# Four plain chunks, an early norm and tables in pieces: a change at the start of a two-layer decoder trunk

## The chip, the cores and the metric

The kernel runs on one core of a Trainium2 chip. The metric is device time in microseconds (us) of one execution of the whole program; the median over several runs counts. The engines are TensorE (PE, with its weight loads PEld), VectorE (DVE), ScalarE (ACT), GpSimd (POOL) and SyncE (SP). SP, ACT and POOL also issue transfers (DMA). Every engine works through its own queue in order.

## The reference

The reference is a decoder trunk of two layers (D = 1024, sequence 512, float32). Cut to what matters here, a layer is:

```python
h = h + 0.5 * swiglu(rmsnorm(h, ffn1_norm[l]), w_gate, w_up, w_down)   # D_FF = 2816
z = rmsnorm(h, mix_norm[l]) @ w_in[l]                                  # four mixers on slices of z:
h = h + concat[MLA(z), SpatialGate(z), HGRN2(z), Retention(z)] @ w_out[l]
h = h + 0.5 * swiglu(rmsnorm(h, ffn2_norm[l]), w_gate, w_up, w_down)
h = h + (p[l] @ w_proj) * sigmoid(rmsnorm(h, ple_norm[l]) @ w_gate)
```

with `swiglu(x) = (silu(x @ w_gate) * (x @ w_up)) @ w_down`, and a final rmsnorm. MLA and Retention turn their queries and keys by sines and cosines of the positions; these are the tables of this study.

## The kernel before

**Layout and number format.** The residual stream lies transposed, as eight tiles `h[k]` of 128 x 512. Each float32 operand is split into a high part (a cast on ACT, L138 or L219) and a low part (a subtraction on DVE, L139 or L220); a product is three matmuls, high-high, high-low and low-high (L190 to L192, function `mm3`). So each weight block costs a load, a cast and a subtraction ahead of its matmuls.

**Feed-forward stage** (`ffn`, L360). Four such stages, two in each layer. D_FF is worked off in 22 chunks of 128 columns, in groups of 4, 4, 4, 4 and 6. A chunk computes gate and up, then silu(gate) times up times the norm's factor, and splits that into `hid`. Most chunks (class `Chunk`, L372) compute gate and up together by a scheme of seven half-width products (named 1 to 7, method `go`) in place of eight, on weight sums made by `seven` (L160) and on the right factors, sums and differences of halves of the normed input that `Right.add` (L275) makes through `Norm.add7` (L323). Product 1 uses only the plain input. The seven weight blocks of a chunk come from four loads: `s1` and `s3` (256 KB each, and POOL adds a second block to each while loading, L174 and L175), `raw` (512 KB, tile `wr`) and `a22` (256 KB). A chunk of seven products is 84 matmuls of 256 columns. The first two chunks of the program are plain: 48 matmuls of 512 columns each, gate into one bank of PSUM and up into another (L428 to L440). Their epilogue starts at L435, where DVE multiplies the bank by the norm's factor `r` into a tile `g` and so frees the bank; Silu (L436) and three DVE steps follow. There are four banks for these products (tag `d`): chunks 0 and 1 hold all four.

**Down products** (`downs`, L413). From the second group on, the products with w_down of the group before (12 matmuls of 512 columns for each of eight `m`) are put between the products of the chunks (`step`), one or two or three to a chunk.

**The start** (L1136 to L1175). `h[k]` and the weights of chunk 0 are loaded in turns on SP, in an order written out by a chain (`inturn`), then the weights of chunk 1, then the constants `cs`. The loads of the seven-product chunks of the first stage wait for `cs` (`start[1]`). The sum of squares for the norm grows on the way (L336 to L343); its last step is at 20.19 us. After that the program has the eight `add7` calls for the right factors and then `ffn`, whose first line is the norm: `norm.scale()` casts the sum (L243), subtracts (L244), adds over the partitions with two matmuls (L247), and takes the inverse root by Ln, Exp (L258, L259) and one Newton step on DVE (L236 to L238).

**Tables** (`tables`, L484). Called once, in the first stage, after chunk 9 (L462). It loads the positions (`pin`), casts them to a side tile `posf`, makes three sines (`sine`, L490: nine steps on DVE and one Sin on ACT each, L493 to L501), loads two decay tables (`dec`, L513), makes four products (L516), and some masks.

**What sets the order.** The program is written as one long text; a planner at build time gives each engine its queue. An instruction's rank is its place in the text, and what stands under `urgent()` ranks 6000 places earlier (weights, their splits, the norm, the chunk's copies out of PSUM). Of the instructions whose inputs and tiles are there, the first in rank goes first. Tiles come from rings with a fixed number of places, named by a tag; the tiles of one tag are handed out in the order of the text, each as soon as a place is free. Rings that matter here: `t` (six places of 128 x 512: `xg` of the right factors, `g` and `u` of the chunks, `a22`, the norm's `ac`, `rv` and `rt`, all temporary tiles of the tables), `side` (four places: `s1`, `s3`, `posf`), `w` (six split weight tiles), `st` (four, also split weights) and `raw` (three). `after` and `inturn` add an order between two instructions without a wait for data.

## Time and profile before

| | us |
|---|---|
| median of 3 runs | 2148.11 (2147.02 to 2150.12) |
| profiled execution | 2146.84 |
| its span in the profile | 2145.1 |
| PE busy | 2078.9 |
| DVE busy | 1599.0 |
| ACT busy | 1061.8 |
| POOL busy | 171.1 |

The profile is one execution. The difference between the span and the execution's own time, 1.7 us, lies outside the recorded instructions. A row of the timeline gives start, duration, engine, line of the kernel, operation, the tile written and the tiles read, the shapes and a count; in brackets stands how long the engine was idle before and what released it. A row of a stretch gives busy time and count for each engine, then the granted clock of PE (1.00 is full), the busy share of the DMA engines and their GB/s. Matmuls overlap, so the distance of their starts tells more than their durations. The same holds, less strongly, for DVE and ACT.

### The profile page before, as it was taken

What the parts mean: (1) busy time and instruction counts of PE and PEld (TensorE: products, weight loads), DVE (VectorE), ACT (ScalarE), POOL (GpSimd) and SP (SyncE); (2) the same over time, 40 slices, a digit from 0 to 9 for tenths busy, and PEclk for the clock granted to TensorE, in tenths of its full rate; (3) what the DMA queues carried; (4) which work ended last, traced back from release to release, by engine and by line L of the source; (5) the groups of instructions that cost most, each with busy time, mean ns of one, the idle gap of its engine ahead of it and who ended that gap; (6) DMA issues with size and microseconds to landing.
All of it is one profiled execution on the core that took longest, in us unless ns stands there. A gap on an engine that the chain in (4) does not pass through costs nothing.

```text
span 2145.1 us, 36254 instructions
## 1 busy us (share of the span) xinstructions
PE 2078.9 (97%) x14336; PEld 1821.7 (85%) x14336; DVE 1599.0 (75%) x2720; ACT 1061.8 (50%) x1897; POOL 171.1 (8%) x217
## 2 busy tenths in 40 slices
PE   6997999999999999999989999999999999999997
PEld 5996999877678999998889999988776889998987
DVE  7778776776678877777897776777765887777676
ACT  7443444643566544444664444455445664444452
POOL 1101110001000111110010111000010010011000
PEclk8998999999999999999999999999999999999999
DMA  6635563323234655564355566432222465565341
GB/s 190 154 122 146 138 156 85 113 82 95 64 89 118 163 152 153 147 153 111 116 143 152 145 157 153 121 101 95 66 89 69 114 153 152 143 154 151 98 132 52
DMA packets 119561, 267.47 MB, mean 125 GB/s; under 512 B 13024, under 2 KB 17632, under 8 KB 119392
## 3 DMA queue, kind: packets, MB, share of 16 engines
q1 hardware_dynamic: 90928, 215.15, 31.7%
q0 software_dynamic: 25792, 47.20, 13.7%
q10 hardware_dynamic: 2672, 2.82, 0.4%
q8 instruction: 112, 1.84, 0.4%
q14 instruction: 57, 0.47, 0.1%
HBM read 260.92 MB, written 2.10 MB: 123 GB/s over the span
## 4 chain that ended last, share of the span: by engine, by line
PE 87%; DVE 6%; DMA 3%; ACT 3%; issue 1%; SPq 0%; ACTq 0%; DVEq 0%
PE dn L190 8%; PE dn L192 7%; PE gx L190 7%; PE gx L192 7%; PE gx L191 7%; PE dn L191 7%; PE gy L190 5%; PE gy L191 5%; PE gy L192 5%; PE z L190 3%; PE z L191 3%; PE z L192 3%; DMA wr<-in_wgu 1%; PE y L190 1%; PE y L192 1%; PE y L191 1%
## 5 line engine op out<-in xcount | busy, mean ns | idle before, releaser
L138 ACT CAST ws<-wr 128x512 fp32r<-128x512 f32 x344 | 210.6, 621 | 386.4 <-DMA wr<-in_wgu 191.3
L190 PE MATMUL gx<-b,ws 128*128 128x256 f32 x1296 | 368.7, 285 | 19.2 <-ACT g L389 9.1
L191 PE MATMUL gx<-b,ws 128*128 128x256 f32 x1296 | 367.3, 283 | 0.0
L192 PE MATMUL gx<-b,ws 128*128 128x256 f32 x1296 | 367.1, 283 | 0.0
L139 DVE TENSOR_TENSOR ws<-wr,ws 128x512 fp32r<-128x512 f32 x344 | 233.9, 688 | 134.3 <-ACT ws L138 133.7
L139 DVE TENSOR_TENSOR wl<-wr,wh 128x1024 fp32r<-128x1024 f32 (+3 forms) x197 | 222.4, 1131 | 149.0 <-PE gy L192 78.9
L138 ACT CAST wh<-wr 128x1024 fp32r<-128x1024 f32 (+3 forms) x197 | 191.9, 975 | 198.6 <-PE z L191 63.2
L190 PE MATMUL dn<-hid,wh 128*128 128x512 f32 x704 | 281.0, 399 | 0.9 <-ACT wh L138 0.5
L192 PE MATMUL dn<-hid,wl 128*128 128x512 f32 x704 | 279.3, 398 | 0.0
L191 PE MATMUL dn<-hid,wh 128*128 128x512 f32 x704 | 275.0, 392 | 0.0
L190 PEld LDWEIGHTS gx<-b,ws 128*128 128x128 f32 x1296 | 248.8, 192 | 27.0 <-ACT u L393 10.0
L190 PE MATMUL gy<-b,ws 128*128 128x256 f32 x872 | 249.3, 286 | 5.4 <-DVE g L398 4.1
L191 PEld LDWEIGHTS gx<-b,ws 128*128 128x128 f32 x1296 | 248.8, 192 | 3.5
L191 PE MATMUL gy<-b,ws 128*128 128x256 f32 x872 | 248.0, 284 | 1.7 <-DVE b L139 1.7
L192 PEld LDWEIGHTS gx<-b,ws 128*128 128x128 f32 x1296 | 248.8, 192 | 0.1
L192 PE MATMUL gy<-b,ws 128*128 128x256 f32 x872 | 247.1, 284 | 1.3 <-DVE ws L139 1.3
L190 PEld LDWEIGHTS gy<-b,ws 128*128 128x128 f32 x872 | 168.4, 193 | 8.0 <-DVE g L398 4.7
L191 PEld LDWEIGHTS gy<-b,ws 128*128 128x128 f32 x872 | 168.5, 193 | 3.3 <-DVE b L139 1.9
L192 PEld LDWEIGHTS gy<-b,ws 128*128 128x128 f32 x872 | 168.1, 193 | 2.9 <-DVE ws L139 1.5
L192 PEld LDWEIGHTS dn<-hid,wl 128*128 128x128 f32 x704 | 132.3, 188 | 34.4 <-DVE wl L139 3.3
L190 PEld LDWEIGHTS dn<-hid,wh 128*128 128x128 f32 x704 | 132.8, 189 | 33.1 <-ACT wh L138 8.1
L191 PEld LDWEIGHTS dn<-hid,wh 128*128 128x128 f32 x704 | 132.9, 189 | 24.9
(379 smaller groups left out, 4260.3 us busy)
## 6 DMA issues: line engine op xcount, KB each, us to landing
s<-in_wgu SPq DMA_DIRECT2D x172, 256.0 KB, 2.8
wr<-in_wgu SPq DMA_DIRECT2D x86, 512.0 KB, 4.4
s<-in_wgu POOLq DMA_DIRECT2D x172, 256.0 KB, 4.9
wr<-in_wdn SPq DMA_DIRECT2D x64, 512.0 KB, 4.8
a<-in_wgu SPq DMA_DIRECT2D x86, 256.0 KB, 4.3
wr<-in_winT SPq DMA_DIRECT2D x40, 512.0 KB, 3.5
wr<-in_wdn SPq DMA_DIRECT2D x32, 384.0 KB, 3.2
wr<-in_winN SPq DMA_DIRECT2D x16, 512.0 KB, 3.5
```

Of the source, the lines that this page charges most:

```text
L138: i = act.copy(hi, src)
L139: dve.tensor_tensor(lo, src, hi.bitcast(F32), op=ALU.subtract)
L190: i = pe.matmul(o, lhsT=a[0], rhs=b[0], start=start, stop=False, skip_group_check=go_on)
L191: pe.matmul(o, lhsT=a[0], rhs=b[1], start=False, stop=False, skip_group_check=go_on)
L192: pe.matmul(o, lhsT=a[1], rhs=b[0], start=False, stop=stop, skip_group_check=go_on)
```

## The change

1. **Four plain chunks.** In the first stage of the program chunks 0 to 3 are plain, not only 0 and 1. Chunks 2 and 3 load and split their gate and up blocks by `weights` (512 KB each, two blocks a chunk); the cast of chunk 2's second block is put behind the norm's Exp on ACT (`late`). The loads have no wait of their own. In `seven` the argument `late` goes away.
2. **The norm ahead of the right factors.** `norm.scale()` is called before the `add7` calls; in them, for this first norm alone, the scaled copy `xg` is put behind the norm's Exp on ACT. `ffn` takes the result from `norm.r`.
3. **Tables in pieces.** `tables` becomes a generator, of which the stage takes a piece after each odd chunk from 5 on: the sine for MLA, the cosine, its two products with the decay, the sine, its two products, the masks. A sine has its own load and cast of the positions; `posf` goes away, and the decay tables are loaded twice. The memset of the upper half of `tabM` moves to the start.
4. **a22 in the ring of the sums.** `a22` is taken from `side`, which gets five places; `t` gets five.

```diff
     def t2(shape=(P, T), dt=F32, name="t"):
-        return tp.tile(list(shape), dt, tag="t", bufs=6, name=nm(name))
+        return tp.tile(list(shape), dt, tag="t", bufs=5, name=nm(name))
...
+    tabs = {"m": cp.tile([P, T], F32, name="tabM")}
+    pool.memset(tabs["m"][0:64], 1.0)
...
     def side(shape=(P, T), name="sd"):
-        return tp.tile(list(shape), F32, tag="side", bufs=4, name=nm(name))
+        return tp.tile(list(shape), F32, tag="side", bufs=5, name=nm(name))
...
-    def weights(src, cols=WB, keep=False, two=False, one=False):
+    def weights(src, cols=WB, keep=False, two=False, one=False, late=None):
...
-            parts(hi[:, :cols], lo[:, :cols], raw[:, :cols])
+            inturn(parts(hi[:, :cols], lo[:, :cols], raw[:, :cols]), late)
             return hi, lo
 
-    def seven(a1, a2, wait=None, late=None):
+    def seven(a1, a2, wait=None):
...
-            s1, s3, raw, a22 = side(name="s1"), side(name="s3"), rtile(), t2(name="a22")
+            s1, s3, raw, a22 = side(name="s1"), side(name="s3"), rtile(), side(name="a22")
...
-            for p, src in ((7, s3), (4, a22)):
-                inturn(keep(p, src), late)
+            keep(7, s3)
+            keep(4, a22)
             dve.tensor_tensor(r2, r2, r1, op=ALU.add)
-            inturn(keep(3, r2), late)
+            keep(3, r2)
...
             g = t2(name="xg")
-            act.activation(g, h[k], AF.Copy, scale=gain(self.gi, k))
-            if plain is None:
+            i = act.activation(g, h[k], AF.Copy, scale=gain(self.gi, k))
+            if plain is not None:
+                after(i, self.exp)
+            else:
                 self.square(k)
...
-        r = norm.scale()
+        r = norm.r or norm.scale()
...
-                if start and f < 2:
+                if start and f < 4:
                     o = []
                     for m in range(2):
                         o.append(start[0].pop(0) if f == 0 else dense("gu"))
-                        for k in range(KD if f else 0):
-                            mm3(o[m], wpart(start[2][m], k * P), xpart(norm.x[k]), k == 0, k == KD - 1)
+                        if f > 0:
+                            w = start[2][m] if f == 1 else weights(wgu[idx, f, m], late=norm.exp if f == 2 and m else None)
+                            for k in range(KD):
+                                mm3(o[m], wpart(w, k * P), xpart(norm.x[k]), k == 0, k == KD - 1)
...
-                if f == 9 and hook is not None:
-                    hook()
+                if hook is not None and f % 2:
+                    next(hook, None)
...
+    def sine(dst, p0, inv, phase, turn):
+        q = slice(p0, P)
+        pin, a, n = t2((P, T), I32, name="pin"), t2(name="ang"), t2(name="turn")
+        nc.scalar.dma_start(out=pin, in_=pos)
+        pick = lambda c: cs[q, c:c + 1] if isinstance(c, int) else c
+        a, n, dst = a[q], n[q], dst[q]
+        dve.tensor_copy(n, pin[q])
+        dve.tensor_scalar(a, n, pick(inv), None, op0=ALU.mult)
...
+        act.activation(dst, a, AF.Sin)
 
     def tables():
...
+        sine(tabs["m"], 64, 0, 1, 2)
+        dve.tensor_scalar(tabs["m"][64:P], tabs["m"][64:P], cs[64:P, 3:4], None, op0=ALU.mult)
+        yield
+        for nme, phase, turn in (("c", 5, 6), ("s", 0.0, 0.0)):
+            for s in "qk":
+                tabs[nme + s] = cp.tile([P, T], F32, name=f"tab{nme}{s}")
+            tq = tabs[nme + "q"]
+            sine(tq, 0, 4, phase, turn)
+            yield
+            for j, s in ((1, "k"), (0, "q")):
+                dt_ = t2(name="dec")
+                nc.scalar.dma_start(out=dt_, in_=dec[j])
+                dve.tensor_tensor(tabs[nme + s], tq, dt_, op=ALU.mult)
+            yield
...
     start[1] = inturn(nc.sync.dma_start(out=cs, in_=cst[:, 0:K_TOP]), prev)
+    norm.scale()
     for k in PAIRED:
         norm.add7(k, norm.x)
     for l in range(L):
         nxt = Norm(4 * l + V_MIX)
-        ffn(2 * l, norm, nxt.add, *((start, tables) if l == 0 else ()))
+        ffn(2 * l, norm, nxt.add, *((start, tables()) if l == 0 else ()))
```

More of the change, by code (lines that the diff above doesn't have):

```diff
@@ L165, in keep @@
             w[p] = (wtile("ws") if n else spare("ws"))[:, 0:WB].rearrange("p (e c) -> p e c", e=2)
-            return parts(w[p][:, 0], w[p][:, 1], src)
+            parts(w[p][:, 0], w[p][:, 1], src)
         with urgent():
-            s1, s3, raw, a22 = side(name="s1"), side(name="s3"), rtile(), t2(name="a22")
+            s1, s3, raw, a22 = side(name="s1"), side(name="s3"), rtile(), side(name="a22")
             r1, r2 = raw[:, 0:T], raw[:, T:WB]
@@ L316, in __init__ @@
             self.x = [None] * KD
-            self.acc = None
+            self.acc = self.r = None
         def add(self, k):
@@ L375, in __init__ @@
             def __init__(self, f):
-                late = norm.exp if start and f == 2 else None
-                self.w = seven(wgu[idx, f, 0], wgu[idx, f, 1], start and start[1], late)
+                self.w = seven(wgu[idx, f, 0], wgu[idx, f, 1], start and start[1])
                 X, yz = dense("gx"), dense("gy")
@@ L479, in ffn @@
             done(m)
-    tabs = {}
-    def tables():
-        pin = t2((P, T), I32, name="pin")
-        posf = side(name="posf")
-        nc.scalar.dma_start(out=pin, in_=pos)
-        dve.tensor_copy(posf, pin)
-        def sine(dst, inv, phase, turn):
-            a, n = t2(name="ang"), t2(name="turn")
-            dve.tensor_scalar(a, posf, inv, None, op0=ALU.mult)
-            dve.tensor_scalar(n, a, 1.0 / TWO_PI, turn, op0=ALU.mult, op1=ALU.add)
-            dve.tensor_scalar(n, n, MAGIC, None, op0=ALU.add)
-            dve.tensor_scalar(n, n, MAGIC, None, op0=ALU.subtract)
-            for c in (C1, C2, C3):
-                dve.scalar_tensor_tensor(a, n, -c, a, op0=ALU.mult, op1=ALU.add)
-            dve.tensor_scalar(a, a, phase, PI_LO, op0=ALU.add, op1=ALU.min)
-            dve.tensor_scalar(a, a, -PI_LO, None, op0=ALU.max)
-            act.activation(dst, a, AF.Sin)
-        tm = cp.tile([P, T], F32, name="tabM")
-        sine(tm, cs[:, 0:1], cs[:, 1:2], cs[:, 2:3])
-        dve.tensor_scalar(tm, tm, cs[:, 3:4], None, op0=ALU.mult)
-        pool.memset(tm[0:64], 1.0)
-        tabs["m"] = tm
-        co, si = t2(name="co"), t2(name="si")
-        sine(co, cs[:, 4:5], cs[:, 5:6], cs[:, 6:7])
-        sine(si, cs[:, 4:5], 0.0, 0.0)
-        for j, s in enumerate("qk"):
-            dt_ = t2(name="dec")
-            nc.scalar.dma_start(out=dt_, in_=dec[j])
-            for nme, src in (("c", co), ("s", si)):
-                tb = cp.tile([P, T], F32, name=f"tab{nme}{s}")
-                dve.tensor_tensor(tb, src, dt_, op=ALU.mult)
-                tabs[nme + s] = tb
@@ new lines, in sine @@
+    def sine(dst, p0, inv, phase, turn):
[6 more added lines that the diff above has]
+        dve.tensor_scalar(a, n, pick(inv), None, op0=ALU.mult)
+        dve.tensor_scalar(n, a, 1.0 / TWO_PI, pick(turn), op0=ALU.mult, op1=ALU.add)
+        dve.tensor_scalar(n, n, MAGIC, None, op0=ALU.add)
+        dve.tensor_scalar(n, n, MAGIC, None, op0=ALU.subtract)
+        for c in (C1, C2, C3):
+            dve.scalar_tensor_tensor(a, n, -c, a, op0=ALU.mult, op1=ALU.add)
+        dve.tensor_scalar(a, a, pick(phase), PI_LO, op0=ALU.add, op1=ALU.min)
+        dve.tensor_scalar(a, a, -PI_LO, None, op0=ALU.max)
+        act.activation(dst, a, AF.Sin)
```

## The prediction

> **What bounds the kernel now.** I read the page first (engines, chain), then the list of PE's waits, then busy time by stretches, then the start and the stage of the tables in order of time.
>
> ```profile
> PE 2078.9 (97%) x14336; PEld 1821.7 (85%) x14336; DVE 1599.0 (75%) x2720; ACT 1061.8 (50%) x1897; POOL 171.1 (8%) x217
> PE 87%; DVE 6%; DMA 3%; ACT 3%; issue 1%; SPq 0%; ACTq 0%; DVEq 0%
> ```
>
> PE is 97% busy and sets the end; it is idle for 66 of 2145.1 us. The longest waits of PE:
>
> ```profile
> PE ms L247 <- ACT ac L243: 9.2, 1, 9.2
> PE gx L190 <- ACT g L389: 9.1, 2, 8.2
> PE gx L190 <- DVE g L435: 6.6, 1, 6.6
> ```
>
> The first and the third make one pause at the start; the second lies in the stage of the tables. Stretches of the start (busy time of PE, PEld, DVE, ACT, POOL, granted clock, DMA share, GB/s), and a full stretch to compare:
>
> ```profile
> 0.00:25.00 25.00, 23.17 (x100) 17.26 (x101) 16.74 (x30) 18.85 (x34) 4.51 (x12) 1.00 0.92 295
> 28.90:46.47 17.57, 1.58 (x2) 0.57 (x2) 17.21 (x39) 12.46 (x26) 1.75 (x3) 0.57 0.38 87
> 46.47:52.02 5.55, 5.55 (x26) 5.55 (x27) 4.67 (x9) 4.71 (x9) 0.85 (x1) 0.52 0.39 61
> 100.00:125.00 25.00, 25.00 (x172) 23.08 (x171) 16.98 (x27) 11.41 (x21) 2.60 (x3) 1.00 0.52 144
> ```
>
> From 28.90 to 46.47 PE does two small matmuls while DVE is busy for 17.21 of 17.57 us: **the pause at the start is DVE's work**, not a transfer. Behind it the clock is at half: 26 matmuls take 5.55 us.
>
> **The start, part by part.** PE's end of chunk 1 and start of chunk 2, then five matmuls around a gap in the stage of the tables, which show the distance of their starts:
>
> ```profile
> 28.28 0.39 PE L191 MATMUL gu<-x,wh 128*128 128x512 f32 x1
> 28.51 0.39 PE L192 MATMUL gu<-x,wl 128*128 128x512 f32 x1
> 46.47 0.58 PE L190 MATMUL gx<-x,ws 128*128 128x256 f32 x1 [6.58 <-DVE g L435]
> ...
> 166.09 0.28 PE L191 MATMUL gy<-x,ws 128*128 128x256 f32 x1
> 166.21 0.28 PE L192 MATMUL gy<-x,ws 128*128 128x256 f32 x1
> 167.74 0.51 PE L192 MATMUL gy<-b,ws 128*128 128x256 f32 x1 [1.25 <-DVE ws L139]
> 168.25 0.41 PE L191 MATMUL gy<-b,ws 128*128 128x256 f32 x1
> 168.47 0.41 PE L192 MATMUL gy<-b,ws 128*128 128x256 f32 x1
> ```
>
> 512 columns take 0.23, 256 columns 0.12, and 0.21 at half clock. The 26 behind the pause lose 5.55 - 26 x 0.12 = 2.4. What releases chunk 2 is L435, the first step of chunk 0's epilogue, which frees a bank of sums:
>
> ```profile
> 20.19 0.69 DVE L343 TENSOR_TENSOR acc<-acc,sq 128x512 f32<-128x512 f32 x1
> 33.13 0.68 DVE L139 TENSOR_TENSOR b<-xg,b 128x512 fp32r<-128x512 f32 x1
> 33.74 0.41 DVE L294 SCALAR_TENSOR_TENSOR xg<-xg,xg 128x256 f32<-128x256 f32 x1
> 34.07 0.42 DVE L139 TENSOR_TENSOR b<-xg,b 128x256 fp32r<-128x256 f32 x1
> 34.50 1.42 ACT L326 ACTIVATE xg<-h,vec 128x512 f32<-128x512 f32 x2
> 37.47 0.62 ACT L243 CAST ac<-acc 128x512 fp32r<-128x512 f32 x1
> 41.38 0.63 ACT L259 ACTIVATE r<-rt 128x512 f32<-128x512 f32 x1
> 44.19 0.69 DVE L238 SCALAR_TENSOR_TENSOR r<-rt,r 128x512 f32<-128x512 f32 x1
> 45.73 0.69 DVE L435 TENSOR_TENSOR g<-gu,r 128x512 f32<-128x512 f32 x1
> L139 DVE TENSOR_TENSOR wl<-wr,wh 128x1024 fp32r<-128x1024 f32 (+3 forms) x197 | 222.4, 1131 | 149.0 <-PE gy L192 78.9 <-ACT wh L138 36.1 <-ACT g L391 29.8
> ```
>
> The sum of squares is ready at 20.88, but the norm begins at 37.47, behind the last two xg at 34.50: ring t is handed out in program order, and the right factors stand first. The change turns this round, so r comes early. But chunk 0's g is a tile of the same ring that comes after all eight xg, and on DVE its step stands behind theirs. So I count what DVE does before L435, at the distance of starts seen in these rows: 0.60 for 512 columns, 0.33 for 256, 1.13 for 1024.
>
> - The norm takes 4.5 us from 37.47 to the end of Exp at 42.01. It starts at 20.9 plus a shift. Chunk 2's first block (512 KB) has no wait on its load, so SP may issue it ahead of the other first loads (0.52 MB at 295 GB/s: 1.8 us; the DMA engines are at 0.92 there, so they don't hide it), and its split (1.1 on DVE) comes ahead of the last squares. Bounds 0 and 2.9; I take 2.0, nearer to the upper, since the share of 0.92 leaves little room. Exp ends at 27.4.
> - The new wait: the first xg stands behind Exp on ACT, and behind it the casts of the right factors, for which DVE waits; this is why DVE's work starts only there. The second block of chunk 2 is cast behind Exp too; PE wants it 5.5 us (24 x 0.23) after the first.
> - DVE after Exp: three norm steps 1.8; the low halves of two more plain blocks 2.3; the right factors, four times six of 0.33 and one of 0.60, 10.4; the first sums of chunks 4 and 5, three each and urgent, 3.6. Together 18.1; the last two right-factor steps (0.9) may follow L435. So L435 starts at 27.4 + 17.2 = 44.6 and PE at 45.3, 1.2 before 46.47. Bounds: 30.0 if L435 follows r at once (27.4 + 1.8 + 0.7, and a hand-over), 52.5 if the other twelve urgent steps for chunks 4 and 5 come first too (7.2). I stay between the two: these need weight tiles which the plain blocks hold, while the right factors need only ACT, as in the 17.21 busy us above.
> - Chunks 2 and 3 take 96 x 0.227 = 21.8 in place of 168 x 0.12 = 20.2: +1.6. The half clock behind the pause stays.
> - Two split chunks go, with six loads of 256 KB, two of 512 and four summing ones, 14 casts on ACT and 18 steps on DVE; four loads of 512 KB and four splits come in. On SP these pass ahead of chunk 4's sums, on POOL chunk 4's take the place of chunk 2's. That relieves DVE after 46 us, where PE is full anyway: 0; without that cover nothing is lost, since work goes away.
>
> Start: -1.2 + 1.6 = **+0.4**.
>
> **The tables.** PE's matmuls into dn, then gx, then gy, each for a full stretch and for the stage of the tables:
>
> ```profile
> 100.00:150.00 50.00, 14.55 (x59) 10.33 (x58) 3.41 (x5) 1.00 0.39 112
> 150.00:200.00 50.00, 16.42 (x65) 12.49 (x64) 3.42 (x5) 0.80 0.57 144
> ...
> 100.00:150.00 50.00, 21.44 (x168) 20.98 (x168) 1.25 (x3) 3.70 (x10) 1.00 0.39 112
> 150.00:200.00 50.00, 12.24 (x72) 11.56 (x72) 0.84 (x2) 1.77 (x5) 0.80 0.57 144
> ...
> 100.00:150.00 50.00, 17.25 (x132) 16.58 (x132) 3.97 (x7) 1.00 0.39 112
> 150.00:200.00 50.00, 9.24 (x48) 8.65 (x48) 1.50 (x3) 0.80 0.57 144
> ```
>
> At full clock the first stretch is worth 59 x 0.23 + 300 x 0.12 = 49.6 us, the second 65 x 0.23 + 120 x 0.12 = 29.4. The stage loses **20.2 us**, idle and half clock together. Ring t is the cause again: all tables are one block of the program, so chunk 10's tiles of t are handed out after the last table's. What the tables cost DVE (steps on ang; L495; L496) and what they wait for:
>
> ```profile
> 155.00:195.00 40.00, 11.32 (x21) 1.89 (x3) 0.75 0.61 150
> L495 DVE TENSOR_SCALAR turn<-turn 128x512 f32<-128x512 f32 x3 | 1.6, 531 | 0.0
> L496 DVE TENSOR_SCALAR turn<-turn 128x512 f32<-128x512 f32 x3 | 1.2, 414 | 0.0
> DVE posf L488 <- DMA pin<-in_pos: 1.1, 1, 1.1
> DVE tabcq L516 <- DMA dec<-in_dec: 4.5, 1, 4.5
> ```
>
> After the change a sine is one piece of three tiles, pin, turn and ang, and pin is free after its cast. With the chunk's c and u and the next chunk's c that makes five held at once, as many as t then has. Its DVE work is 14.1/3 = 4.7 us. Pieces come every second chunk; two chunks are 2 x 84 x 0.12 + 48 x 0.23 = 31 us of PE, in which DVE is idle for a third (16.98 busy of 25), some 10 us: a piece fits. Two more loads of pin and two of dec (1 MB), issued on ACT's queue ahead of the next chunk's casts, lie beside full PE with ACT busy 11.41 of 25; uncovered they would cost the waits counted next. What stays is DVE, in order, standing before a late load: 3 x 1.1 + 2 x 4.5 = 12.3. Bounds 0 and 12.3; I take 2.0, nearer to none, as DVE has those 10 us and the next chunk's first weights are ready a chunk ahead. Tables: -20.2 + 2.0 = **-18.2**.
>
> The Trainium skill ("TensorE: Matmul & The Clock Gate", "What's actually happening") has the clock fall to half after a window of about 3.4 us of idle. By that rule the three waits of 1.1 would cost 3.3 at most. The row at 167.74 disagrees: after a wait of 1.25 the starts are 0.21 apart; with some 15 such matmuls (0.09 each) they would cost 7.4.
>
> **Edits put at nothing.** a22 leaves t for the ring of the sums: three tiles a chunk out of five, not two out of four. A sum's two transfers:
>
> ```profile
> s<-in_wgu SPq DMA_DIRECT2D x172, 256.0 KB, 2.8
> s<-in_wgu POOLq DMA_DIRECT2D x172, 256.0 KB, 4.9
> ```
>
> 7.7 us stand against 10.1 us of PE in a chunk without downs (84 x 0.12) and 15.6 with: a tile freed a chunk earlier is in time, by 2.4 at the least. Half a chunk late would cost 2.6 in one or two chunks of each of four feed-forward stages, some 16; as the spare has both signs, 0. Ring t of five in the mixers: PE is full there; an estimate from one DVE step of 0.60 at some six places where a sixth tile is missed gives +4, and a22's place, which t no longer gives away, -2. The memset of tabM on POOL lies ahead of its first sum.
>
> Sum: 2146.84 + 0.4 - 18.2 = 2129.0. The profiled execution lies 1.27 under the median 2148.11, so **2130.3**.
>
> **Rivals.**
> - *Both pauses go* (0.20). L435 follows r, PE starts at 30.0 with a full clock: 15.3 + 2.4 less, 2112.6. For it: L435 needs only r and a bank. Against: the order of the ring, by which the norm itself stood 16.6 us (20.88 to 37.47).
> - *The dec pieces still stop PE* (0.15): 2 x (4.5 + 1.4 of half clock) = 11.8 in place of 2.0: 2140.1. For it: the row of 4.5. Against: weights lie ready.
> - *Five pauses for one*, slower (0.08). The next chunk's c comes after the piece in t; if it waits for the whole piece, product 6 and all behind it stand. A sine piece takes 4.5 + 4.7 + 0.6, a dec piece 4.5 + 1.4: 3 x 9.8 + 2 x 5.9 = 41.2, less products 1 and 5 (24 x 0.12 = 2.9) each time: 26.7, and 5 x 2.4 of half clock: 38.7. 2130.3 - 2.0 + 38.7 = 2167. It decides from 4 us a piece (20.2/5). Against: pin's place is free before c is due.
> - *No net change* (0.05): the ring of the sums takes 16 back: 2146.
>
> **How the numbers follow.** The forecast has 0.52. The time is 2130; the range of 2112 to 2143 takes in the first two rivals and leaves out the last two. Measurement tells 0.2% (4.3 us) from no change: faster 0.52 + 0.20 + 0.15 less 0.01, 0.86; same 0.05; slower 0.09.
>
> **What would show it.** Right: the norm (L243) near 23; chunk 2's first matmul near 45 and DVE full ahead of it; no stretch of 25 us between 60 and 300 with PE under 24. Wrong: chunk 2 near 30 (first rival); PE idle before product 6 of chunks 6, 8, 10, 12, 14 (five pauses); DVE waiting 4.5 at L516 with PE idle (second); PE's waits spread over all four feed-forward stages (ring of the sums).

## The result, and the profile after

The changed kernel takes 2182.82 us (median of 4 runs, 2180.89 to 2186.33) beside 2147.76 for the kernel before: a ratio of 1.0163, with a 95% interval from 1.0146 to 1.0181. It is slower by 35 us. The prediction was 2130.

The page of the kernel after, engines first, then three rows of the DMA issues (size of one, median time from issue to landing):

```profile
PE 2091.8 (96%) x14264; PEld 1823.0 (84%) x14264; DVE 1591.6 (73%) x2702; ACT 1051.8 (48%) x1881; POOL 166.4 (8%) x213
...
wr<-in_wgu SPq DMA_DIRECT2D x88, 512.0 KB, 4.9
s<-in_wgu SPq DMA_DIRECT2D x168, 256.0 KB, 2.7
s<-in_wgu POOLq DMA_DIRECT2D x168, 256.0 KB, 5.1
```

The first of these rows in the kernel before:

```profile
wr<-in_wgu SPq DMA_DIRECT2D x86, 512.0 KB, 4.4
```

DVE and ACT do less than before and PE issues fewer matmuls, and yet the span is longer. The sums' own transfers are hardly slower (2.7 and 5.1 us against 2.8 and 4.9); the raw blocks (wr) land 0.5 us later by the median. PE's waits in the kernel after (us in total, times, longest):

```profile
PE gu L193 <- DVE g L441: 19.8, 1, 19.8
PE dn L195 <- DVE wl L142: 13.5, 10, 1.8
PE gx L193 <- ACT u L397: 11.1, 18, 1.6
PE gy L193 <- DVE g L405: 9.6, 14, 2.1
PE nr L693 <- issue: 4.4, 2, 2.2
```

The start pause is still there, now as one wait. The long waits of the tables are gone. In their place stand many waits of one or two us: for the low part of a block of w_down (dn), and for the epilogues of the chunks (u, g). PE's list of the kernel before has no wait for wl, and for u it has this row:

```profile
PE gx L190 <- ACT u L393: 7.4, 9, 1.8
```

The last row of the kernel after, in front of the small products of the mixers, was not there before.

Where they lie is read from stretches cut at the last down product of each feed-forward stage and at the first seven-product matmul of the next (busy time of PE, PEld, DVE, ACT, POOL, clock, DMA share, GB/s). The kernel before: first feed-forward stage, mixers, and the other three feed-forward stages:

```profile
0.00:398.70 398.70, 366.20 (x2327) 330.88 (x2328) 297.15 (x500) 191.52 (x346) 38.80 (x51) 0.95 0.52 141
398.70:674.20 275.50, 273.51 (x2133) 212.57 (x2133) 200.05 (x370) 145.87 (x259) 13.94 (x23) 1.00 0.30 88
674.20:1029.20 355.00, 350.38 (x2380) 322.65 (x2379) 265.33 (x435) 170.56 (x310) 35.63 (x42) 1.00 0.55 144
1084.30:1443.10 358.80, 351.15 (x2380) 322.79 (x2379) 270.70 (x444) 174.81 (x316) 34.02 (x39) 1.00 0.54 139
1718.60:2074.20 355.60, 350.29 (x2380) 322.56 (x2380) 265.91 (x433) 170.59 (x309) 32.62 (x38) 1.00 0.53 139
```

The same stretches of the kernel after:

```profile
0.00:393.50 393.50, 362.87 (x2255) 323.98 (x2256) 289.64 (x482) 184.60 (x330) 34.49 (x47) 0.97 0.53 141
393.50:673.20 279.70, 275.54 (x2134) 213.80 (x2133) 200.51 (x371) 146.32 (x261) 13.00 (x22) 0.99 0.31 87
673.20:1041.00 367.80, 354.77 (x2380) 324.62 (x2379) 265.16 (x435) 169.49 (x309) 36.44 (x43) 1.00 0.54 139
1096.00:1465.00 369.00, 356.13 (x2380) 326.02 (x2380) 270.99 (x445) 172.55 (x315) 34.79 (x40) 0.99 0.51 134
1743.00:2109.40 366.40, 354.52 (x2380) 324.26 (x2379) 265.49 (x433) 169.61 (x308) 33.04 (x39) 1.00 0.52 134
```

The first stage gains 5.2 us. The three later feed-forward stages, whose text the change touches only through the rings, lose 12.8, 10.2 and 10.8. The mixers of the two layers lose 4.2 (in the rows) and 2.5. Nearly all of the loss lies in the three later feed-forward stages, and not where the start and the tables were rebuilt.

### The profile page after: what moved, and what is told of

Read it like the earlier page. It is cut to its first block, busy times and chain, and to the rows that moved or that the text cites. A ratio compares the mean times of both kernels' runs of the same rounds, so it can differ in the third digit from the quotient of the medians.

```text
span 2180.5 us, 36139 instructions
## 1 busy us (share of the span) xinstructions
PE 2091.8 (96%) x14264; PEld 1823.0 (84%) x14264; DVE 1591.6 (73%) x2702; ACT 1051.8 (48%) x1881; POOL 166.4 (8%) x213
## 5 line engine op out<-in xcount | busy, mean ns | idle before, releaser
L141 ACT CAST ws<-wr 128x512 fp32r<-128x512 f32 x336 | 205.9, 619 | 414.1 <-DMA wr<-in_wgu 238.6
L193 PE MATMUL gx<-b,ws 128*128 128x256 f32 x1272 | 364.0, 286 | 15.4 <-ACT u L397 11.1
L194 PE MATMUL gx<-b,ws 128*128 128x256 f32 x1272 | 360.5, 283 | 0.7 <-DVE b L142 0.7
L195 PE MATMUL gx<-b,ws 128*128 128x256 f32 x1272 | 360.3, 283 | 0.0
L142 DVE TENSOR_TENSOR ws<-wr,ws 128x512 fp32r<-128x512 f32 x336 | 229.0, 688 | 170.1 <-ACT ws L141 169.2
L142 DVE TENSOR_TENSOR wl<-wr,wh 128x1024 fp32r<-128x1024 f32 (+3 forms) x201 | 227.1, 1133 | 143.1 <-PE gy L195 73.4
L195 PE MATMUL dn<-hid,wl 128*128 128x512 f32 x704 | 280.1, 399 | 13.5 <-DVE wl L142 13.5
L193 PEld LDWEIGHTS gx<-b,ws 128*128 128x128 f32 x1272 | 243.9, 192 | 26.9 <-ACT u L397 15.5
L194 PEld LDWEIGHTS gx<-b,ws 128*128 128x128 f32 x1272 | 244.1, 192 | 4.5 <-DVE b L142 1.1
L195 PEld LDWEIGHTS gx<-b,ws 128*128 128x128 f32 x1272 | 244.2, 192 | 0.2
L177 POOL DMA_DIRECT2D s<-in_wgu x84 | 72.8, 867 | 1268.4 <-DMA s<-in_wgu 276.3
L193 PEld LDWEIGHTS dn<-hid,wh 128*128 128x128 f32 x704 | 132.8, 189 | 31.8 <-ACT wh L141 7.0
```

Of the source, the lines that this page charges most:

```text
L141: i = act.copy(hi, src)
L142: dve.tensor_tensor(lo, src, hi.bitcast(F32), op=ALU.subtract)
L177: nc.gpsimd.dma_start(out=s1, in_=a2[:, T:WB], accum_op=ALU.add)
L193: i = pe.matmul(o, lhsT=a[0], rhs=b[0], start=start, stop=False, skip_group_check=go_on)
L194: pe.matmul(o, lhsT=a[0], rhs=b[1], start=False, stop=False, skip_group_check=go_on)
L195: pe.matmul(o, lhsT=a[1], rhs=b[0], start=False, stop=stop, skip_group_check=go_on)
```

## Experiment 1: each part alone

Four kernels. The ring edit alone, in the kernel before:

```diff
-        return tp.tile(list(shape), dt, tag="t", bufs=6, name=nm(name))
+        return tp.tile(list(shape), dt, tag="t", bufs=5, name=nm(name))
...
-        return tp.tile(list(shape), F32, tag="side", bufs=4, name=nm(name))
+        return tp.tile(list(shape), F32, tag="side", bufs=5, name=nm(name))
...
-            s1, s3, raw, a22 = side(name="s1"), side(name="s3"), rtile(), t2(name="a22")
+            s1, s3, raw, a22 = side(name="s1"), side(name="s3"), rtile(), side(name="a22")
```

> The kernel before with one edit: the fourth weight block a22 comes from the ring of the sums, which has five buffers instead of four, and ring t has five instead of six. Start, norm and tables are those of before. Theory A (the ring of the sums is what costs: a chunk now takes three of five buffers, so the loads of its sums can start only 1.67 chunks ahead instead of two, and they bunch with the other weight loads): the three later FFN stages lose what they lost in the changed kernel, about 16 + 9 + 11 us, and the first one about 10, so some 45 us over the kernel before (2185 to 2200), with TensorE waiting for VectorE's low parts of wdn and for the epilogues in all four FFN stages. Rival B (the losses come from the order that the new start and the table pieces leave behind, not from the ring): within 10 us of the kernel before.

Measured: 2194.7, a ratio of 1.0204 (1.0180 to 1.0229) to the kernel before of the same runs, 2148.5. Of its 46 us by the medians (44 by the ratio) some 8 are the pause for the tables, which the ring edit made longer (one wait of 16.1 us for g, where the kernel before has 8.2).

The changed kernel with these three lines taken back:

> The changed kernel with the ring edit taken back: a22 from ring t of six buffers, the ring of the sums with four. The four plain chunks, the early norm and the five table pieces stay. Theory A: the later FFN stages go back to their lengths of before (416, 414 and 356 us), the table gain of about 18 us stands and the start costs about 5 (first product of chunk 2 at 52 us against 46.5, plus two plain chunks): about 2135, faster than the kernel before by 0.5%. Rival B: the losses stay, about 2175.

Measured: 2143.8, ratio 0.9982 (0.9964 to 1.0000). Without the ring edit the rest of the change is worth about 4 us, at the edge of what these runs tell from nothing, and the ring edit costs 39 on top of it. Between the traces of this kernel and of the changed one the four feed-forward stages differ by 5, 13, 10 and 11 us, and the rest by 1 in all.

The kernel before with the tables in pieces (the generator `tables`, the new `sine`, and the call `next(hook, None)` after each odd chunk), and nothing else:

> The kernel before with the tables in five pieces and nothing else. The prediction's term for this part was -18.2 us: 2129.5, with no stretch between 150 and 200 us in which TensorE stands. The rival 'the products with the decay tables still stop TensorE' gives 2140, 'five pauses for one' 2167.

Measured: 2138.1, ratio 0.9947 (0.9929 to 0.9965): a gain of 11, not of 18.

The kernel before with the four plain chunks and the early norm, and nothing else:

> The kernel before with four plain chunks and the norm ahead of the right factors, and nothing else (tables in one go after chunk 9, rings as before). By the prediction's term +0.4 us: 2148. By the trace of the changed kernel the start pause grew from 17.6 to 19.9 us, begins 3.4 us later, and two plain chunks take 1.6 us more than two of seven products: some +5 us, 2153, if VectorE still comes to the epilogue of chunk 0 only at 51 us for reasons of its own order; if that lateness was the ring of the sums (loads of chunk 5's block late), 2148.

Measured: 2160.1, ratio 1.0045 (1.0029 to 1.0062): a loss of 10.

The parts alone give +44, -11 and +10 by their ratios, together +42 against +35 measured; the 8 us of longer pause, which tables in pieces do not have, are of the size of the difference. Theory A's claim that the ring edit carries the loss holds. How it does so is the next question.

## Experiment 2: how the ring of the sums costs

First, where a22 lies. In one kernel a22 got a buffer of its own:

```diff
-        return tp.tile(list(shape), dt, tag="t", bufs=6, name=nm(name))
+        return tp.tile(list(shape), dt, tag="t", bufs=5, name=nm(name))
...
-            s1, s3, raw, a22 = side(name="s1"), side(name="s3"), rtile(), t2(name="a22")
+            s1, s3, raw = side(name="s1"), side(name="s3"), rtile()
+            a22 = tp.tile([P, T], F32, tag="a22", bufs=1, name=nm("a22"))
```

> The kernel before, with a22 in a buffer of its own (one buffer), ring t of five, and the ring of the sums with its four buffers for s1 and s3 alone: the same ten buffers in all as in the changed kernel, but s1 and s3 may again be loaded two chunks ahead. Theory A (the ring of the sums, shared by three tiles a chunk, lets the sums' loads start only 1.67 chunks ahead, where they bunch with the loads of the raw block): 2141 to 2158, the loss of 44 us gone. Rival C (ring t with five buffers instead of six is what costs): about 2190, as in the run with the ring edit alone. Rival D (a22's own early load is what gets in the way of the raw block, whatever its ring): 2165 to 2180.

In another it shares the ring of the sums, left at four buffers:

```diff
-            s1, s3, raw, a22 = side(name="s1"), side(name="s3"), rtile(), t2(name="a22")
+            s1, s3, raw, a22 = side(name="s1"), side(name="s3"), rtile(), side(name="a22")
```

> The kernel before, with a22 from the ring of the sums, that ring left at four buffers and ring t at six. Theory A: the lead falls from 1.67 to 1.33 chunks (5.3 us less at a chunk of 16), so the loss grows well beyond 44 us: 2240 to 2330. Rival C (ring t of five costs): no loss, about 2150. Rival D (a22's early load): a22 is loaded later here, so no more than in the run with five buffers, 2165 to 2195.

Measured: 2168.2 with a buffer of its own (ratio 1.0081, 1.0052 to 1.0111) and 2201.1 with the ring of four (1.0237, 1.0204 to 1.0270), beside 2147.6. Theory A in its simple form misses both times: with the lead restored 17 to 20 us of loss stay, and with a third of a chunk less lead the time is 2201 where the theory wanted 2240 or more. Both times lie nearer to rival D's ranges, though 2201 is above them.

Neither run is a clean test of the lead, though. With the buffer of its own 6 of the 20 us are a longer pause for the tables (14.2 us for g against 8.2), and ring t has five places, which costs some 7 by a run below. The run with the ring of four has ring t of six, so its 2201 can't be set beside the 2194.7 of the ring edit alone. And there the sums do come late: ACT waits 74.6 us in all for s1 and s3 (12.7 in the kernel before, 27.7 with the ring edit alone), while the raw blocks land at a median of 4.4 as before. So there is more than one cause, and late sums are one of them.

Three kernels on the base of 2143.8 (the change without its ring edit) and one on the changed kernel take these apart. The first swaps two loads on SP and moves no instruction of a computing engine:

```diff
-            inturn(nc.sync.dma_start(out=s1, in_=a2[:, 0:T]), wait)
-            inturn(nc.sync.dma_start(out=s3, in_=a1[:, 0:T]), wait)
+            i3 = inturn(nc.sync.dma_start(out=s3, in_=a1[:, 0:T]), wait)
+            inturn(nc.sync.dma_start(out=s1, in_=a2[:, 0:T]), i3)
```

> The changed kernel with its ring edit taken back (2143.8 us), and SyncE's loads of each chunk's s1 and s3 swapped: s3 first, then s1. Nothing else moves: the order of work on TensorE, VectorE and ScalarE is the same to the last instruction. s3's buffer comes free some 10 us after s1's, so s1 is loaded some 10 us later than in the kernel before, as it is in the changed one. Theory A (the later loads of the sums cost): a loss of 15 to 25 us, 2159 to 2169, and TensorE waits for VectorE's low parts of wdn as in the changed kernel. Theory O (what costs is the order that a22's early readiness leaves on ScalarE, VectorE and TensorE, not the loads): 2141 to 2148.

The second has ring t at five buffers, and a22 still in it:

> The changed kernel with a22 back in ring t and the ring of the sums at four, but ring t left at five buffers. Theory C (ring t of five has its own part, as a22, the epilogues' and the tables' tiles come from it): 2152 to 2165. Theories A and O, by which all of the loss comes with a22's move: 2141 to 2148.

The other two move the splits of products 4 and 3 (`keep(4, a22)`, the sum r2 and `keep(3, r2)`) into a function that is called behind the copy of product 1:

```diff
-                        act.copy(self.c[:, A], o)
+                        self.w.pop("tail")(act.copy(self.c[:, A], o))
```

once with a22 in a buffer of its own and four buffers for s1 and s3,

> The changed kernel with a22 in a buffer of its own and four buffers for s1 and s3 (no sharing), and the splits of products 4 and 3 ordered behind ScalarE's copy of product 1, about where they stood when a22 came late. Theory O: with the loads two chunks ahead again and the split of a22 back behind that copy, nothing is left of the loss: 2143 to 2150. If the order of that one split has no part in it, the loss of the run with a buffer of its own stays (20 us, of which 6 were a longer pause for the tables, absent here): 2156 to 2162.

and once in the shared ring of five:

> The changed kernel, its shared ring of five as it is, with the splits of products 4 and 3 ordered behind ScalarE's copy of product 1. Theory O: gains what that order cost, 12 to 16 us, 2167 to 2171; with theory A alone: no gain, 2180 to 2186.

Measured, beside 2147.4: loads swapped 2152.5 (1.0022, 1.0009 to 1.0035); ring t of five 2150.5 (1.0016, 0.9998 to 1.0034); own buffer and split put back 2153.1 (1.0025, 1.0011 to 1.0040); shared ring and split put back 2178.7 (1.0140, 1.0104 to 1.0176). So on the base of 2143.8 a load of s1 that comes 10 us later costs some 9 us, less than theory A's 15 to 25, and ring t of five some 7 (its interval just touches that of the base). Putting the split back gains 4 in the shared ring, within the uncertainty, where theory O wanted 12 to 16: the order on ACT is at most a small part. The last pair is the clearest: ten buffers in both, the split in the same place in both, and **sharing the ring alone costs 25 us**, with intervals that do not touch; the own buffer leaves 9 over the base, and ring t of five, with its 7, is about as large.

What sharing does is seen in one chunk, chunk 10 of the second feed-forward stage. It is one of the slow ones: by the median a raw block lands 0.5 us later than before. Rows of the timeline (start, duration, engine, line, operation, tiles, idle time before and its releaser), kernel after:

```profile
797.25 0.33 SPq L174 DMA_DIRECT2D s<-in_wgu  x1
798.57 0.33 SPq L175 DMA_DIRECT2D s<-in_wgu  x1
802.67 0.33 SPq L176 DMA_DIRECT2D wr<-in_wgu  x1
...
800.93 0.87 POOL L177 DMA_DIRECT2D s<-in_wgu  x1 [6.25 <-DMA s<-in_wgu]
801.74 0.95 POOL L178 DMA_DIRECT2D s<-in_wgu  x1
...
809.16 0.62 ACT L141 CAST ws<-wr 128x512 fp32r<-128x512 f32 x1 [5.11 <-DMA wr<-in_wgu]
...
813.88 1.22 DVE L142 TENSOR_TENSOR wl<-wr,wh 128x1024 fp32r<-128x1024 f32 x1
...
815.15 0.50 PE L195 MATMUL dn<-hid,wl 128*128 128x512 f32 x1 [1.78 <-DVE wl L142]
```

The same chunk in the kernel before:

```profile
791.53 0.33 SPq L172 DMA_DIRECT2D s<-in_wgu  x1
796.88 0.33 SPq L173 DMA_DIRECT2D wr<-in_wgu  x1
...
794.67 0.87 POOL L175 DMA_DIRECT2D s<-in_wgu  x1 [7.55 <-DVE hid L217]
...
800.88 0.62 ACT L138 CAST ws<-wr 128x512 fp32r<-128x512 f32 x1 [2.56 <-DMA wr<-in_wgu]
...
805.60 1.22 DVE L139 TENSOR_TENSOR wl<-wr,wh 128x1024 fp32r<-128x1024 f32 x1
```

Before, the buffers of s1 and s3 of the next chunk come free some 9 us apart (their loads start at 782.35 and 791.53), and one sum is under way when the raw block (wr) is issued: the cast starts 4.0 us after the issue (796.88 to 800.88). After, s1 and s3 are loaded within 1.3 us, both of GpSimd's sums start within 0.8 us just ahead of the raw block, and the cast starts 6.5 us after the issue (802.67 to 809.16). ACT waits 5.11 for it instead of 2.56. ACT and DVE work in order. The w_down block has its high part cast right behind the late cast (809.69), and its low part wl starts on DVE 4.7 us behind that late cast, like before (813.88, 805.60); PE stands 1.78 for it. **The block that is late here is not one of the ring's own**; it is the raw block, which is in flight together with them.

If so, keeping s1's load behind the raw block should help, although it makes s1 later still. Two kernels, both on the changed one. The first adds an order on SP:

```diff
-            inturn(nc.sync.dma_start(out=s1, in_=a2[:, 0:T]), wait)
+            inturn(inturn(nc.sync.dma_start(out=s1, in_=a2[:, 0:T]), wait), block[0])
...
-            inturn(nc.sync.dma_start(out=raw, in_=a1), wait)
+            block[0] = inturn(nc.sync.dma_start(out=raw, in_=a1), wait)
```

> The changed kernel, rings as they are, with one order more for SyncE: the load of a chunk's s1 is issued only behind the load of the raw block of the chunk ahead of it. The order of work on TensorE, VectorE and ScalarE stays that of the changed kernel but for a few instructions at the start. Theory K (what costs in the shared ring is that s1, s3, a22 and the two sums of GpSimd are in flight together with the raw block of the chunk ahead, which so lands late: median 5.5 us in the chunks from the seventh on, against 4.3): the raw block's landing goes back to about 4.4 us, and 10 to 20 us come back, 2162 to 2173. Theory A (the sums are late): s1 comes some 5 us later still, so it gets worse, 2188 to 2200.

The second issues the loads of s1, s3 and a22 on GpSimd (`nc.gpsimd.dma_start`), so that SP never stands at the shared ring:

> The changed kernel, rings as they are, with the loads of s1, s3 and a22 issued by GpSimd instead of SyncE, so that SyncE, which works in order, never stands at the shared ring: raw blocks and the blocks of wdn no longer queue behind it. Theory S (the wait for a buffer of the shared ring on SyncE holds up the raw blocks and the wdn blocks behind it): most of the loss comes back, 2150 to 2165. Theory K (transfers in flight together): no gain, 2178 to 2190, or worse.

Measured, beside 2149.4: raw block first 2171.8 (1.0121, 1.0085 to 1.0158); loads on GpSimd 2175.1 (1.0129, 1.0100 to 1.0159). ACT's idle time ahead of its splits of the raw block, and what ended it, goes with this. The change without its ring edit, then own buffer and split put back, the changed kernel, and the raw block first:

```profile
L141 ACT CAST ws<-wr 128x512 fp32r<-128x512 f32 x336 | 205.5, 620 | 380.4 <-DMA wr<-in_wgu 197.1
```

```profile
L141 ACT CAST ws<-wr 128x512 fp32r<-128x512 f32 x336 | 205.9, 620 | 399.8 <-DMA wr<-in_wgu 213.6
```

```profile
L141 ACT CAST ws<-wr 128x512 fp32r<-128x512 f32 x336 | 205.9, 619 | 414.1 <-DMA wr<-in_wgu 238.6
```

```profile
L141 ACT CAST ws<-wr 128x512 fp32r<-128x512 f32 x336 | 206.0, 620 | 408.9 <-DMA wr<-in_wgu 207.4
```

And of PE's waits with the raw block first:

```profile
PE dn L197 <- DVE wl L142: 2.6, 2, 2.3
```

With one order more, 31 of the 41 us that the ring edit adds to ACT's wait for raw blocks are gone (238.6 to 207.4, with 197.1 as the floor), PE's wait for wl falls from 13.5 to 2.6, and 11 us of time come back by the medians (the two intervals just overlap, so the size is loose; the direction is that of theory K, and against theory A). In the two traces the gain lies where the loss was: from the first seven-product matmul to the last down product the three later feed-forward stages take 361.1, 363.6 and 360.3 us in place of 367.4, 368.6 and 366.0 (the profiled execution is the fastest of its four, so by the medians it is less). With the loads on GpSimd 8 come back, which is neither theory: SP at the ring is at most a part of it. That run is not clean: its start changed too (PE waits 12.7 us for GpSimd's first memset), and although chunk 2 begins at 52.16 there and at 52.09 in the changed kernel, its first feed-forward stage is 6 us longer.

What stays open: raw blocks 11, late sums 9, ring t 7 and perhaps 4 for the place of a22's split make 31 of the 39 us. The sizes come from different bases and need not add up, and where the other 8 lie no run says.

## Experiment 3: the tables

The kernel before without the making of the tables: GpSimd fills them with a constant at the start, the sines, scalings and products with the decay are left out.

> The kernel before without the making of the five position tables: they are filled with a constant by GpSimd at the start, so what is left out is their sines, scalings and products with the decay table (the masks stay). It gives the floor under any way of spreading them. Theory G (the prediction's term: what the tables cost before is the 20.2 us that TensorE loses between 150 and 200 us, and five pieces still cost 2.3 us each where they land): 2128, some 10 below the run with the tables in pieces alone. Rival H (what the pieces leave is no cost of theirs, the FFN stage is bound by something else as soon as the tables are out of the way): 2137, the same as in pieces.

Measured: 2125.0, ratio 0.9889 (0.9856 to 0.9921): 23 us under the kernel before, 13 under the pieces. So the pieces do cost something themselves, and theory G holds. PE's waits between 50 and 400 us in the kernel with the tables in pieces alone:

```profile
PE dn L195 <- DVE wl L142: 3.3, 2, 2.1
PE gx L193 <- ACT g L394: 2.2, 2, 1.3
PE gy L193 <- DVE g L404: 2.1, 2, 1.0
PE gx L193 <- ACT u L396: 1.4, 2, 0.9
PE gx L193 <- DVE g L401: 1.1, 3, 0.8
```

and without tables:

```profile
PE gx L195 <- ACT u L398: 0.2, 1, 0.2
```

Eleven short waits, 10.1 us together, each by the lateness of a split or an epilogue on DVE or ACT, stand against 0.2. A finer cut did not help. In the best kernel so far (next section) the tables were cut into eleven pieces, one after each chunk from the fifth on, with a `yield` inside `sine` and one after each product:

> The kernel with the rings of before, four plain chunks and the right factors behind chunk 1's epilogue (2131.2 us), with the tables cut into eleven pieces, one after each chunk from the fifth on, instead of five after each odd chunk. Theory P (each of the five pieces is a lump of 6 to 8 us of VectorE that makes the low part of a wdn block or an epilogue some 2 us late; half as long a lump fits): 8 to 10 us come back, 2121 to 2124. Theory Q (the work itself costs, however it is cut, since VectorE has no room left in these chunks): 2129 to 2133.

Measured: 2131.7 (0.9924, 0.9898 to 0.9950) against 2131.2 uncut: theory Q. A smaller lump in more chunks costs the same, so it is not the size of a lump. What is left is all that the tables bring beside the chunks: the work on DVE and ACT, the loads, and the places in ring t; no run takes these apart.

## Experiment 4: the start

The pause in the kernel after as one stretch, and five rows of its timeline:

```profile
32.33:52.09 19.76, 0.01 (x1) 0.01 (x1) 16.84 (x38) 12.81 (x26) 2.62 (x3) 0.61 0.55 130
```

```profile
28.29 0.69 DVE L257 TENSOR_SCALAR rv<-ms 128x512 f32<-128x512 f32 x1 [2.72 <-PE ms L250]
29.73 0.63 ACT L262 ACTIVATE r<-rt 128x512 f32<-128x512 f32 x1
42.37 0.69 DVE L142 TENSOR_TENSOR ws<-wr,ws 128x512 fp32r<-128x512 f32 x1 [2.92 <-ACT ws L141]
51.02 0.41 DVE L297 SCALAR_TENSOR_TENSOR xg<-xg,xg 128x256 f32<-128x256 f32 x1
51.35 0.68 DVE L441 TENSOR_TENSOR g<-gu,r 128x512 f32<-128x512 f32 x1
```

The norm's Exp ends at 30.4, and the epilogue of chunk 0 (L441), for which PE waits, comes 21 us later, right behind the last step of the right factors (L297). DVE stood for 2.92 of this, until ACT had chunk 5's raw block.

One kernel, the change without its ring edit, writes the right factors behind the epilogue of chunk 1 in the program:

```diff
-    for k in PAIRED:
-        norm.add7(k, norm.x)
+    first_norm = norm
+    start.append(lambda: [first_norm.add7(k, first_norm.x) for k in PAIRED])
...
                     hid.append(split(t, name="hid"))
+                    if f == 1:
+                        start[3]()
```

> The changed kernel with its ring edit taken back (2143.8 us when run alone), and the right factors written behind the epilogue of chunk 1 in the program instead of ahead of chunk 0's. Theory E (the start pause lasts until 50 us because VectorE does the 17 us of right factors and the splits of chunks 4 and 5 between the norm, ready at 33.5 us, and the epilogue of chunk 0, for which the first product of chunk 2 waits): the epilogue comes at about 34 us, TensorE stands 2 to 3 us instead of 18, and the time falls by 13 to 17 us to 2127 to 2131. Rival F (the right factors then come late for chunk 4: 17 us of them and some 12 us of epilogues and splits from 34 us on, against 22 us of plain products): half of the gain is lost in front of chunk 4, 2134 to 2138.

Measured: 2131.2 beside 2147.6, ratio 0.9917 (0.9885 to 0.9948), 12.6 under its base of 2143.8. Its epilogue and PE's first product of chunk 2:

```profile
34.22 1.28 DVE L441 TENSOR_TENSOR g<-gu,r 128x512 f32<-128x512 f32 x2
...
34.95 0.50 PE L193 MATMUL gu<-x,wh 128*128 128x512 f32 x1 [3.02 <-DVE g L441]
```

Theory E: the pause is 3.0 us in place of 19.8 in the changed kernel, and the right factors are in time for chunk 4; PE waits 1.3 us in front of it, for an epilogue (L441). The time is at theory E's upper end.

## Experiment 5: a pause in the mixers that hangs on the place in the program

Every kernel with four plain chunks has two waits of 2 us for "issue" in front of the small products nr, one in each layer's mixers; no kernel with two plain chunks has them. Four plain chunks have 72 matmuls and as many weight loads fewer ahead of this point (14264 of each in the whole program against 14336). The next kernel puts 36 of each back, as matmuls of 32 columns among the warming ones at the start, where PE waits anyway. That is half of the 144 instructions, so they do not stand where they stood in the kernel before, as the expectation has it; they stand 72 places further on than in the kernel without the 36.

```diff
     for _ in range(20):
         pe.matmul(o[:, 0:2 * P], lhsT=wide[:, 0:P], rhs=wide, start=True, stop=True)
+    for _ in range(36):
+        pe.matmul(o[:, 0:32], lhsT=wide[:, 0:P], rhs=wide[:, 0:32], start=True, stop=True)
```

> The kernel with the right factors behind chunk 1's epilogue (2131.2 us), with 36 more matmuls of 32 columns among the warming ones at the start, where TensorE waits for its first blocks anyway. Four plain chunks have 72 instructions of TensorE fewer than two plain ones and two of seven products; with the 36 matmuls and their weight loads every later instruction of TensorE stands at the same place of its instruction stream as in the kernel before. Theory I (the pause of some 2 us in front of the small products nr of both mixers, which every kernel with four plain chunks shows and no other, is a late piece of the instruction stream, and hangs on that place): the two pauses go, and with the half clock behind them 6 us, 2123 to 2127. Rival (the pause comes from the work itself in the mixers, or from when it is reached): they stay, 2129 to 2134.

Measured: 2123.5 beside 2150.2, ratio 0.9886 (0.9856 to 0.9917), 7.6 under the same kernel without them. The mixers of both layers in that kernel, and in the one without the 36 matmuls:

```profile
373.20:648.80 275.60, 273.64 (x2133) 212.47 (x2132) 200.03 (x370) 145.77 (x259) 13.82 (x23) 1.00 0.31 88
1420.20:1695.80 275.60, 273.63 (x2133) 212.51 (x2132) 202.03 (x364) 144.16 (x256) 13.74 (x23) 1.00 0.31 88
```

```profile
372.90:652.30 279.40, 275.33 (x2134) 213.74 (x2132) 200.14 (x370) 145.81 (x259) 13.82 (x23) 0.99 0.30 87
1425.00:1704.40 279.40, 275.20 (x2132) 213.73 (x2131) 202.10 (x364) 144.16 (x256) 13.75 (x23) 0.99 0.31 86
```

275.6 is what the kernel before takes there. 3.8 us in each layer, 7.6 in all, go when the later instructions of PE move by 72 places.

The kept traces show what the pause is. In all eleven kernels that have it, the same number of recorded instructions of PE stands ahead of it: 5313 in the first layer and 19649 in the second, while the time at which PE goes on differs (431 to 463 us, and 1483 to 1523). And in all 22 pauses a transfer of the kind "instruction" (16 KB, on DMA queue q8) starts within 0.5 us of PE's stop, and PE goes on 1.2 to 1.6 us after it has landed. In the kernel after it starts at 449.59, PE's last small product ahead of the pause at 449.36. In the seven kernels without the pause the same transfer, the 20th of its queue in the first layer, starts 6.7 to 14.4 us before PE reaches that place (at 438.3 for 452.7 in the kernel before). So a piece of PE's instruction stream comes late, and theory I holds. What lets the transfer start so late no run shows; the place falls behind 128 small products, four large ones and 25 to 30 small ones in the kernels with the pause, and inside the run of 128 in the others.

This kernel is the best of the study: 1.1% faster than the kernel before.

## Why the prediction was wrong, by its own steps

**The bound of the kernel** was read rightly: PE sets the end, and what counts is where it stands.

**The ring of the sums, put at nothing with a bound of 16, failed.** The step was "7.7 us stand against 10.1 us of PE in a chunk without downs: a tile freed a chunk earlier is in time, by 2.4 at the least". It asks whether the ring's own tiles come in time. Late sums are one part: a later s1 alone costs 9, although the step gave it 2.4 us to spare. And it does not ask what else is in flight when the freed buffers let five transfers go at once: the raw block comes 2.5 us later in the chunk shown (6.5 against 4.0) and 0.5 by the median, and PE waits at a place that reads none of the ring's tiles. This part is worth up to 11 of the 39; sharing as a whole is worth 25. The count "one or two chunks of each of four stages" fell with it: it makes 4 us a stage, and the three later stages lose 10 to 13 each (in the second one PE waits for wl at 749, 815 and 882, once in each group of four chunks). The rival "no net change" had named the sign for it, waits spread over all four feed-forward stages, and this sign came; its price of 16 was less than half of the 39 measured. Two more costs lay in lines that the prediction took for free: ring t of five, put at -2 to +4 and looked for in the mixers, costs 7, and in the feed-forward stages (8 us by the traces, against none in the mixers), where a22's and the epilogues' tiles come from it; and a22, ready early, has its split placed ahead of a copy on ACT, which may cost 4.

**The tables, -18.2, gave -11.** The 20.2 us of the pause were right: without any tables the kernel is 23 faster, and PE's long waits there are gone in pieces too. The mis-sized term is what the pieces themselves cost, 2.0: the waits in the trace make 10, and the runs 13. "DVE is idle for a third" of two chunks was true, but idle time that lies between dependent steps takes in work only by making the next split or epilogue late.

**The start, +0.4, cost 10.** Part of it are the pauses in the mixers (6.7 us in the stretches of the changed kernel, 7.6 by the last run), of which the prediction had no term. The rest is the start itself: with this part alone chunk 2 began at 49.97, 4.7 after the 45.3 of the forecast. In the changed kernel L441 came at 51.35 instead of 44.6. By its steps: Exp ended at 30.4 (29.73 and 0.63), not 27.4. Of these 3.0 us 1.3 are the norm's start, at 24.2 instead of 22.9, a shift of 3.3 against an upper bound of 2.9; 1.7 are the norm's own length, 6.2 instead of 4.5, because its matmul stands in PE's own queue behind chunk 1's products (DVE waits 2.72 for ms); then the 17.2 us of DVE were right, but DVE also stood 2.92 for a raw block, and the last steps of the right factors (0.9), which the prediction let follow L441, came ahead of it: 17.2 + 2.9 + 0.9 = 21.0. The first rival, L435 right after r, did not happen, but the order that it needs is one edit away, and is worth 12.6.

**The sum.** The other rivals did not come: the products with the decay hold up nothing long, and no piece makes a pause of 10. With 0.09 for slower the prediction had given the side that came too little, above all because the ring of the sums and ring t of five were put at nothing, each for itself, and the pieces nearly so.

## What to carry to other kernels

A ring that seems in time for its own tiles can still cost: ask which transfers the freed buffers will start together, and which block, of any tile, is in flight with them. Mean idle time of an engine is no room for extra work when the idle time lies between steps that others wait for. Where a pause stands behind an epilogue, look first at what the program text puts ahead of it on that engine; here two lines moved won as much as all the work on the tables.

## What the runs showed of the hardware that was not expected

TensorE can stand for its own instructions: 2.0 to 2.8 us from one small product to the next, at the same count of instructions in eleven kernels, with a 16 KB transfer of instructions that starts as TensorE stops (experiment 5). Behind the pause, in the kernel after:

```profile
451.76 0.55 PE L693 MATMUL nr<-q,k 128*32 128x32 f32 x38 [2.21 <-issue]
...
453.31 0.63 PE L195 MATMUL z<-x,wl 128*128 128x512 f32 x1
453.74 0.63 PE L193 MATMUL z<-x,wh 128*128 128x512 f32 x1
```

512 columns take 0.43 from start to start here instead of 0.23, from some 1.5 us after PE resumed: the half clock followed a wait of 2.2 us (granted clock 0.82 from 450 to 455 us, 0.84 from 455 to 460). The Trainium skill ("TensorE: Matmul & The Clock Gate", "What's actually happening") has the clock fall after an idle window of about 3.4 us, in a window that runs freely; the pause here is shorter. The small matmuls ahead of it may count as idle; no run here separates that. With the half clock behind it the pause costs nearly twice its length here: 3.8 us in each mixer for 2.2 of waiting.
